# A two-layer hybrid decoder step on one core: the scale before the shift, the first tiles from x without the shift

## The chip, the cores and the metric

The kernel runs on one core of one Trainium2 chip. The time is device microseconds of one execution. The kernel before took 1080.2 us (median of three runs, 1079.94 to 1081.06).

## The reference, cut to what matters

The step takes 512 prompt rows and 8 sample rows through two layers. The change touches the beginning of the first layer and, through the order of its weights, the modulation of both. In float32:

```python
def rmsnorm(x, g):
    y = xf * rsqrt(mean(xf * xf, axis=-1) + EPS)
    return y * g

def adaln(c, w, b):                       # shift, scale, gate: 1024 columns each
    mod = (silu(c) @ w + b)[:, None, :]
    return split(mod, 3, axis=-1)

def even_layer(x, c, g, aw, ab, w_in, ...):
    shift, scale, gate = adaln(c, aw, ab)
    h = rmsnorm(x, g) * (1 + scale) + shift
    z = h @ w_in                          # 8 x 1024 columns
    bg, cg, xv, ga, q, k, v, gb = split_cols(z, ...)
    ...                                   # short convolution; dilated attention of 16 heads
    out = concatenate([y_a, y_b]) @ w_out
    return x + gate * out
```

The prompt has one vector c, the eight samples have one each, so shift and scale are nine rows. The prompt's row multiplies all 512 positions.

## The kernel before

**Layout.** Everything is kept by feature: a tile has 128 features on the partitions and 520 positions (512 prompt, 8 sample) beside each other. x is eight such tiles, xT[0..7]. A product tile of z is 128 columns of w_in times the eight tiles of h. It is made in full float32 precision by three passes: weights and input are each split into a high half (rounded by ACT, `whi` and the first of each pair in `h0`) and a low half (the difference, made by DVE). For each k in 0..7, `mm3` issues six matrix instructions (three passes, positions 0 to 255 and 256 to 519 apart), so a tile has 48. Product tiles lie in PSUM in a pool of two buffers (`mm`); everything else on PSUM shares four (`aux`). ACT evicts the prompt's part of a tile, DVE the samples' (`sample_z`).

**Modulation.** `ada_load` fetches a 1 MB block of the modulation weights into one of three `big` buffers. Before, a block "ss" holds the shift and the scale of one k. `ada_mm` multiplies it with silu(c) (`scT`, eight products, 16 instructions), ACT copies the rows out (`md`), `ada_fin` transposes them on PE, and DVE reduces them (`m9`) to the columns `mS` (shift) and `mA` ((1 + scale) times the norm's weight).

**The head.** SP issues all loads in the order of the program: c, the eight x tiles, two small tables, then modulation blocks and weight tiles. ACT squares the x tiles, DVE adds the squares, PE multiplies them with a 128 x 128 matrix of 1/1024 (lines 407 to 409), so that every partition has the mean; ACT takes the root, DVE the reciprocal (r0), and POOL multiplies the eight x tiles by it (line 416). The loop over j (lines 422 to 448) then does for each k: the modulation block, `h_hi` and `h_lo` (scale and shift x, split it), and the products of the first two tiles (v and k of head pair 0) with h of k = j - 2.

**The pairs.** `head_pair(p)` makes four tiles for two heads: v, k, gate, q. The weights come in the order `seq`. The attention of pair p is put into the products of pair p + 1 by ticks: a tick is the end of one k of a tile (six instructions), so a tile has eight and a pair 32. `at(n, f)` runs f n ticks later; `put` queues work for PE that runs at one piece a tick from its due tick on. For a pair they are the scores (`score`, four blocks of queries), biased by DVE, made exponentials and normalised by ACT and DVE; the transposes of the weights (`turn`, six groups; ACT copies a high half, DVE makes the low half a tick later); and the products with v (`weigh`, eight). The first scores are due five ticks (`Q0`) after the pair's four tiles, the first transposes 16 ticks after them.

Each engine takes its instructions in the order of the program; what stands behind a waiting one waits too.

## Time and profile before

| | |
|---|---|
| median of three runs | 1080.2 us |
| the profiled execution | 1080.08 us, its span 1078.3 |
| PE busy | 1042.2 us of the span (97%), 8656 instructions |
| DVE, ACT, POOL busy | 638.1, 492.3, 27.4 us |
| moved from and to HBM | 149.40 MB read, 18.65 MB written |
| first two product tiles end | 51.41 us into the span |
| pairs 2 to 6, each | 33.4 us |

A window row shows where an engine is short of work, and the granted clock in it. A row of the chain of waits gives a piece that nothing else could overlap. A group row gives the mean duration of a kind of instruction. A duration counts from an instruction's start to its end; of two behind each other on ACT the second may start about 0.1 us before the first ends.

### The profile page before, as it was taken

What the parts mean: (1) busy time and instruction counts of PE and PEld (TensorE: products, weight loads), DVE (VectorE), ACT (ScalarE), POOL (GpSimd) and SP (SyncE); (2) the same over time, 40 slices, a digit from 0 to 9 for tenths busy, and PEclk for the clock granted to TensorE, in tenths of its full rate; (3) what the DMA queues carried; (4) which work ended last, traced back from release to release, by engine and by line L of the source; (5) the groups of instructions that cost most, each with busy time, mean ns of one, the idle gap of its engine ahead of it and who ended that gap; (6) DMA issues with size and microseconds to landing.
All of it is one profiled execution on the core that took longest, in us unless ns stands there. A gap on an engine that the chain in (4) does not pass through costs nothing.

```text
span 1078.3 us, 21052 instructions
## 1 busy us (share of the span) xinstructions
PE 1042.2 (97%) x8656; PEld 989.0 (92%) x8656; DVE 638.1 (59%) x1468; ACT 492.3 (46%) x890; POOL 27.4 (3%) x45
## 2 busy tenths in 40 slices
PE   3999999999999999999999989999999999999996
PEld 1699999999989999999999989999999999999996
DVE  6556777667786444446344586565647666674443
ACT  4575667656663222223333465435454444333333
POOL 3000000000000000000000040000000000000000
PEclk9999999999999999999999999999999999999999
DMA  9486545665436355352744335272635423225212
GB/s 356 159 271 189 166 143 161 209 185 181 141 129 195 119 198 159 117 170 91 248 160 150 105 118 195 91 253 98 235 123 178 171 96 109 83 81 181 99 70 80
DMA packets 82177, 168.96 MB, mean 157 GB/s; under 512 B 7209, under 2 KB 47241, under 8 KB 79001
## 3 DMA queue, kind: packets, MB, share of 16 engines
q1 hardware_dynamic: 82080, 167.61, 46.6%
q8 instruction: 68, 1.11, 0.4%
q14 instruction: 29, 0.23, 0.1%
HBM read 149.40 MB, written 18.65 MB: 156 GB/s over the span
## 4 chain that ended last, share of the span: by engine, by line
PE 92%; DVE 4%; ACT 2%; DMA 1%; issue 1%; SPq 0%; DVEq 0%; ACTq 0%
PE mm L160 75%; PE aux L160 13%; PE aux L543 2%; DVE t L146 1%; ACT t L140 1%; DVE wlo L146 1%; DMA v<-vdr 1%; PE aux L348 0%; PE aux L1239 0%; DVE t L149 0%; DMA t<-in_x_t 0%; PE aux L463 0%; DVE t L202 0%; PE aux L918 0%; ACT whi L140 0%
## 5 line engine op out<-in xcount | busy, mean ns | idle before, releaser
L160 PE MATMUL mm<-t,whi 128*128 128x256 f32 (+1 forms) x4608 | 764.5, 287 | 7.1 <-ACT t L140 4.9
L160 PEld LDWEIGHTS mm<-t,whi 128*128 128x128 f32 x4608 | 637.3, 189 | 36.2 <-issue 21.9
L160 PE MATMUL mm<-t,wlo 128*128 128x256 f32 (+2 forms) x2304 | 465.7, 282 | 0.0
L160 PEld LDWEIGHTS mm<-t,wlo 128*128 128x128 f32 x2304 | 358.8, 189 | 0.0
L146 DVE TENSOR_TENSOR wlo<-wraw,whi 128x512 fp32r<-128x512 f32 x288 | 192.6, 699 | 52.0 <-ACT whi L140 51.7
L140 ACT ACTIVATE whi<-wraw 128x1024 fp32r<-128x1024 f32 x144 | 151.6, 1053 | 98.1 <-PE mm L160 62.9
L146 DVE TENSOR_TENSOR t<-t,t 128x520 fp32r<-128x520 f32 (+6 forms) x164 | 107.0, 652 | 96.3 <-ACT t L140 94.6
L140 ACT ACTIVATE t<-t 128x520 fp32r<-128x520 f32 (+3 forms) x116 | 70.9, 616 | 166.0 <-DVE t L149 97.8
L140 ACT ACTIVATE t<-aux 128x128 f32<-128x128 f32 (+7 forms) x148 | 67.9, 469 | 115.9 <-PE aux L160 64.8
L140 ACT ACTIVATE t<-mm 128x512 f32<-128x512 f32 (+2 forms) x116 | 56.4, 507 | 114.0 <-PE mm L160 112.5
L146 DVE TENSOR_TENSOR t<-aux,t 128x512 fp32r<-128x512 f32 (+6 forms) x120 | 60.8, 512 | 37.1 <-ACT t L140 32.0
L160 PE MATMUL aux<-t,t 64*128 64x256 f32 (+6 forms) x384 | 56.2, 329 | 0.0
L160 PE MATMUL aux<-t,v 128*128 128x512 f32 (+2 forms) x224 | 49.1, 324 | 0.6 <-DVE t L146 0.6
L521 DVE CUSTOM_DVE_ANT_0 t<-aux,t 128x128 f32<-128x128 f32 (+3 forms) x64 | 28.9, 489 | 31.9 <-PE aux L160 31.4
L160 PEld LDWEIGHTS aux<-t,t 64*128 64x128 f32 (+1 forms) x384 | 41.5, 186 | 5.4
L140 ACT ACT_TABLE_LOAD x32 | 41.1, 1283 | 1.3 <-PEq L1353 0.7
L140 ACT ACTIVATE t<-t,mn 128x128 f32<-128x128 f32 (+3 forms) x64 | 35.4, 554 | 13.3 <-DVE mn L521 13.1
L160 PEld LDWEIGHTS aux<-t,v 128*128 128x128 f32 x224 | 34.4, 188 | 1.9 <-DVE t L146 0.8
L149 DVE SCALAR_TENSOR_TENSOR big<-v,ksc,big 128x256 f32<-128x256 f32 x64 | 27.7, 480 | 10.3 <-ACT big L140 9.9
L350 DVE TENSOR_REDUCE m<-aux 128x18 f32<-128x72 f32 x24 | 5.5, 231 | 45.8 <-PE aux L348 45.8
L143 DVE COPY zs<-mm 128x8 f32<-128x8 f32 x76 | 12.1, 159 | 34.6 <-ACT t L140 33.7
L146 DVE TENSOR_TENSOR t<-mm,t 128x512 f32<-128x512 f32 (+1 forms) x24 | 16.5, 689 | 26.6 <-PE mm L160 17.4
(145 smaller groups left out, 603.2 us busy)
## 6 DMA issues: line engine op xcount, KB each, us to landing
wraw<-in_w_in_e SPq DMA_DIRECT2D x64, 512.0 KB, 6.4
wraw<-in_w_in_o SPq DMA_DIRECT2D x48, 512.0 KB, 3.2
big<-in_ada_e SPq DMA_DIRECT2D x12, 1024.0 KB, 8.3
big<-in_ada_o SPq DMA_DIRECT2D x12, 1024.0 KB, 8.5
wraw<-in_w_out_e SPq DMA_DIRECT2D x16, 512.0 KB, 3.5
big<-in_state_ret SPq DMA_DIRECT2D x16, 512.0 KB, 7.5
out_new_ret_sample<-big SPq DMA_DIRECT2D x16, 512.0 KB, 3.7
wraw<-in_w_out_o SPq DMA_DIRECT2D x16, 512.0 KB, 3.2
```

What stands on the lines that cost most here:

```text
L140: return nc.scalar.activation(out=out, in_=in_, func=func, scale=scale, **kw)
L143: return nc.vector.tensor_copy(out, in_)
L146: return nc.vector.tensor_tensor(out=out, in0=in0, in1=in1, op=op)
L149: return nc.vector.scalar_tensor_tensor(out=out, in0=in0, scalar=scalar, in1=in1, op0=op0, op1=op1)
L160: nc.tensor.matmul(out, lhsT=lhsT, rhs=rhs, start=start, stop=stop)
L350: nc.vector.tensor_reduce(out=m, in_=pt.rearrange("p s (g r) -> p s r g", g=4)[:, :, 0:9, :], op=ALU.add, axis=AX.X)
L521: nc.vector.tensor_tensor_reduce(out=sb, in0=s[:, 0:n], in1=bt[e][:, S - n:S], scale=1.0, scalar=3e38, op0=ALU.add, op1=ALU.min, accum_out=mn,
L543: nc.tensor.transpose(ep[:, c * P:(c + 1) * P], src, ident)
```

## The change

The modulation weights are stored in three parts now, scale, shift and gate, in blocks of two k each. So four blocks give the scale of all eight k, four more the shift.

x is loaded ahead of the rest and squared; the mean is now taken by five products with one column, the root and its reciprocal on 5 columns, and turned back into rows by products of the broadcast column with the identity (`rms_rows`). DVE multiplies each x tile by r0 (`x_normed`). `x_scaled` scales x by `mA` and splits it, without the shift; the first four tiles (pair 0) are made of that (`xa`). The shift blocks are multiplied among the products of the third and fourth tile (`steps`). In pair 1 the raw weights of the first four tiles (kept in `t4` buffers, `raw_of`) are multiplied with the shift (`shift_rows`, `z_shift`), and the result is added to the kept tiles. The four tiles of pair 1 are made of the x without shift too, with ten more columns that hold the shift (`z_second`, 530 instead of 520 columns). During pair 1, `h_x` adds the shift to x in place, and `h_split` splits it anew into the same `xa` buffers, at ticks 8 to 22 and 25 to 32. From pair 2 on everything is as before. The work of pair 0's attention is moved by D0 = 8 ticks.

```diff
-            r = mk(wp, [P, KT, P], F32, "wraw", 4)
+            r = t4().rearrange("p (k c) -> p k c", k=KT) if i < 4 else mk(wp, [P, KT, P], F32, "wraw", 4)
+            raw_of.append(r)
...
+    def rms_sums(sq, n=T):
+        blocks = [c * P for c in range(n // P)] + ([n - P] if n % P else [])
+        pc = aux([P, len(blocks)])
+        for i, c in enumerate(blocks):
+            mm(pc[:, i:i + 1], sq[:, c:c + P], on_d[:, 0:1], True, True)
+        return pc
+    def rms_roots(pc, scale=1.0):
+        rc = mk(cp, [P, 5], F32, "rc", 2)[:, 0:pc.shape[1]]
+        act(rc, pc, ACTF.Sqrt, bias=eps[:, 0:1], scale=scale)
+        nc.vector.reciprocal(rc, rc)
+        return rc
+    def rms_rows(rc, r):
+        pr, n = aux([P, S]), r.shape[1]
+        for i in range(4):
+            mm(pr[:, i * P:(i + 1) * P], rc[:, i:i + 1].to_broadcast([P, P]), ident, True, True)
+        act(r[:, 0:S], pr)
+        if n > S:
+            pr = aux([P, n - S])
+            mm(pr, rc[:, 4:5].to_broadcast([P, P]), ident[:, P - n + S:P], True, True)
+            vcopy(r[:, S:n], pr)
...
+    load(csm[:, 0:P], a["c_small"][:, 0:P])
     xT = [tt() for _ in range(KT)]
     for j in range(KT):
         load(xT[j], a["x_t"][:, j, :])
-    load(csm[:, 0:P], a["c_small"][:, 0:P])
-    load(pv, a["small_t"])
-    raw0 = [ada_load(0, "ss", 0)]
-    w_raw()
-    raw0.append(ada_load(0, "ss", 1))
-    w_raw()
-    raw0.append(ada_load(0, "ss", 2))
+        if j == 1:
+            load(pv, a["small_t"])
...
+    rawA = []
+    for i in range(3):
+        rawA.append(ada_load(0, "scale", i))
+        if i < 2:
+            w_raw()
...
-    for x in xT:
-        nc.gpsimd.tensor_tensor(out=x, in0=x, in1=r0, op=ALU.mult)
...
+    rms_rows(rms_roots(rms_sums(sqa)), r0)
+    def x_normed(j):
+        vtt(xT[j], xT[j], r0, ALU.mult)
+    def x_scaled(j):
+        x, g = xT[j], mA[0][:, j, 8:9]
+        hi, lo = tr(T + 10), tr(T + 10)
+        vtt(xhs[:, j, :], x[:, S:T], mA[0][:, j, 0:NB], ALU.mult)
+        act(hi[:, 0:S], x[:, 0:S], ACTF.Copy, scale=g)
+        act(hi[:, S:T], xhs[:, j, :])
+        stt(lo[:, 0:S], x[:, 0:S], g, f(hi[:, 0:S]), ALU.mult, ALU.subtract)
+        lo_of(lo[:, S:T], xhs[:, j, :], hi[:, S:T])
+        xa.append((hi, lo))
...
+    md = ada_mm(rawA[0])
+    x_normed(0)
+    x_normed(1)
+    ada_fin(0, "scale", 0, md)
+    for i in range(4):
+        for j in (2 * i, 2 * i + 1):
+            x_scaled(j)
+        for _ in range((2, 0, 1, 0)[i]):
             w_hi()
             w_lo()
+        if i == 0:
+            rawA.append(ada_load(0, "scale", 3))
+        else:
+            rawS.append(ada_load(0, "shift", i - 1))
+            w_raw()
+        if i < 3:
+            x_normed(2 * i + 2)
+            x_normed(2 * i + 3)
+            if i:
+                first_two(2 * i)
+            md = ada_mm(rawA[i + 1])
+            first_two(2 * i + 1 if i else 0)
+            ada_fin(0, "scale", i + 1, md)
+            if i == 0:
+                first_two(1)
+        else:
+            first_two(6)
+            first_two(7)
+    for (_, _, m), ps in zip(seq, ps01):
+        z_keep(m, ps)
...
+    def shift_fin(i):
+        ada_fin(0, "shift", i, mdS.pop(i))
+        for j in (2 * i, 2 * i + 1):
+            act(xa[j][0][:, T:T + 10], mS[0][:, j, :])
+            lo_of(xa[j][1][:, T:T + 10], mS[0][:, j, :], xa[j][0][:, T:T + 10])
+        if i < 1:
+            rawS.append(ada_load(0, "shift", 3))
+            w_raw()
+    mdS = {}
+    steps = {
+        (2, 0): [w_hi], (2, 1): [w_lo, lambda: shift_mm(0)], (2, 3): [lambda: shift_fin(0)],
+        (2, 4): [lambda: shift_mm(1)], (2, 6): [lambda: shift_fin(1), w_raw],
+        (2, 7): [lambda: shift_mm(2)], (3, 1): [lambda: shift_fin(2)],
+        (3, 2): [w_hi], (3, 3): [w_lo, lambda: shift_mm(3)], (3, 5): [lambda: shift_fin(3), w_raw],
+        (3, 6): [w_hi], (3, 7): [w_lo],
+    }
+    for t in (2, 3):
+        ps, w = mm2(), take_w(seq[t])
+        for k in range(KT):
+            mm3(ps, w, k, xa[k][0], xa[k][1], k == 0, k == KT - 1)
+            for fn in steps.get((t, k), ()):
+                fn()
+        z_keep(seq[t][2], ps)
...
+    def shift_rows(n):
+        at(1, z_shift, n, rows_mm(scS, raw_of[n].unsqueeze(2)))
+    def z_shift(n, md):
+        m, x = zf[n]
+        ws = rows_turn(md)
+        act(x, x, ACTF.Silu if n == 2 else ACTF.Identity, bias=ws[:, 0, 8:9])
+        vtt(zs[0][:, m, :], zs[0][:, m, :], ws[:, 0, 0:NB], ALU.add)
+    for n in range(4):
+        at(1 + 2 * n, shift_rows, n)
+    h0 = xa
+    def h_x(j):
+        x = xT[j]
+        vtt(x[:, S:T], xhs[:, j, :], mS[0][:, j, 0:NB], ALU.add)
+        act(x[:, 0:S], x[:, 0:S], ACTF.Identity, scale=mA[0][:, j, 8:9], bias=mS[0][:, j, 8:9])
+    def h_split(j):
+        hi, lo = xa[j]
+        act(hi[:, 0:T], xT[j])
+        lo_of(lo[:, 0:T], xT[j], hi[:, 0:T])
+    for j in range(KT):
+        at(8 + 2 * j, h_x, j)
+        at(25 + j, h_split, j)
+    def z_second(m, func=ACTF.Identity):
+        ps = z_tile(0, m, xa, T + 10)
+        x, ws = tt(S), mk(cp, [P, 9], F32, "ws", 2)
+        vcopy(ws, ps[:, 1, T - H0:T - H0 + 9])
+        act(p2(x), ps[:, :, 0:H0], func, bias=ws[:, 8:9])
+        vtt(zs[0][:, m, :], ps[:, 1, H0:H0 + NB], ws[:, 0:NB], ALU.add)
+        return x
...
+        if p == 0:
+            D0 = 8
+            put_fill(v_out, zf[0][1], after=4)
+            at(6, k_made, zf[1][1])
+            st["sg"] = zf[2][1]
+            at(9, lambda: q_made(p2(zf[3][1])))
+            at(7, bias_load)
+            at(11, window_load)
+        elif p == 1:
+            D0 = 0
+            put_fill(v_out, z_second(48 + p), after=2)
+            at(1, k_made, z_second(40 + p))
+            st["sg"] = z_second(56 + p, ACTF.Silu)
+            bias_load()
+            at(5, window_load)
+            q_made(p2(z_second(32 + p)))
...
+            put(score, qb, after=D0 + Q0 + n)
```

The engines' instructions stand in another order at three places. First PE at the start of the program. Before, the four products with the matrix `on_d` come first, then three modulation blocks (`aux<-big`) with their transposes (`aux<-csm,md`), and then the first products with `whi`:

```order
L160 MATMUL aux_159<-t_137,on_d 128x256
L160 MATMUL aux_160<-t_137,on_d 128x264
L160 MATMUL aux_159<-t_157,on_d 128x256
L160 MATMUL aux_160<-t_157,on_d 128x264
L160 MATMUL aux_182<-big_125,scT 32x256 x8
L348 MATMUL aux_195<-csm,md_191 128x128 x2
L160 MATMUL aux_207<-big_129,scT 32x256 x8
L348 MATMUL aux_226<-csm,md_216 128x128 x2
L160 MATMUL aux_240<-big_133,scT 32x256 x8
L160 MATMUL mm_180<-t_222,whi_193 128x256
```

After, on PE at the same place:

```order
L160 MATMUL aux_165<-on_d,t_140 128x1 x5
L160 MATMUL aux_174<-csm,rc_171 128x128 x4
L160 MATMUL aux_180<-csm,rc_171 128x8
L160 MATMUL aux_185<-big_126,scT 32x256 x8
L354 MATMUL aux_198<-csm,md_194 128x128 x2
L160 MATMUL aux_233<-big_130,scT 32x256 x8
L160 MATMUL mm_183<-t_205,whi_219 128x256
```

The first products now follow the second block, and the broadcast of r0 stands ahead of the first.

Second, ACT in pair 1, from the last exponentials of pair 0 up to the eviction of the first transposes. Before (`t_827` and `t_829` are the fourth block's weights of the two heads, `t_898<-aux` is the eviction, `v_850` is the split of v):

```order
L140 ACTIVATE whi_813<-wraw_661 128x1024
L140 ACTIVATE t_763<-t_763,ls_732 128x256
L140 ACTIVATE t_765<-t_765,ls_736 128x256
L140 ACTIVATE t_827,ls_732<-t_827,mn_731 128x512
L140 ACTIVATE t_829,ls_736<-t_829,mn_735 128x512
L140 ACTIVATE t_848<-aux_843 128x512
L140 ACTIVATE v_850<-t_848 128x8x64
L140 ACTIVATE t_827<-t_827,ls_732 128x512
L140 ACTIVATE t_829<-t_829,ls_736 128x512
L140 ACTIVATE t_898<-aux_893 128x512
```

After (`t_1006` and `t_1008` are those weights, `t_114` to `t_116` are x tiles of `h_x`, `t_1020` is the key's split of pair 1):

```order
L140 ACTIVATE whi_990<-wraw_771 128x1024
L140 ACTIVATE t_114<-t_114,mS_88,mA_86 128x512
L140 ACTIVATE t_934<-t_934,ls_891 128x256
L140 ACTIVATE t_936<-t_936,ls_895 128x256
L140 ACTIVATE t_1020<-t_969 128x512
L140 ACTIVATE t_1006,ls_891<-t_1006,mn_890 128x512
L140 ACTIVATE t_1008,ls_895<-t_1008,mn_894 128x512
L140 ACTIVATE t_115<-t_115,mS_88,mA_86 128x512
L140 ACTIVATE t_1006<-t_1006,ls_891 128x512
L140 ACTIVATE t_1008<-t_1008,ls_895 128x512
L140 ACTIVATE t_116<-t_116,mS_88,mA_86 128x512
L140 ACTIVATE t_1074<-aux_1069 128x512
```

Three x tiles and a key split stand among them now; one more x tile (`t_113`) stands between the first exponentials and these rows.

Third, DVE in the same pair, among the low halves of the transposed weights (`t<-aux,t`) and the window scores (`big`). Before, from the first low half to the fifth (`t_973`):

```order
L146 TENSOR_TENSOR t_899<-aux_893,t_898 128x512
L573 TENSOR_REDUCE t_518<-big_649 128x8x2
L146 TENSOR_TENSOR t_921<-aux_915,t_920 128x512
L146 TENSOR_TENSOR big_649<-big_649,v_775 128x1024
L146 TENSOR_TENSOR t_937<-aux_932,t_936 128x384
L573 TENSOR_REDUCE t_518<-big_649 128x8x2
L146 TENSOR_TENSOR wlo_964<-wraw_675,whi_929 128x512
L146 TENSOR_TENSOR t_956<-aux_951,t_955 128x384
L146 TENSOR_TENSOR wlo_964<-wraw_675,whi_929 128x512
L146 TENSOR_TENSOR t_947<-t_902,t_946 128x512
L146 TENSOR_TENSOR t_973<-aux_967,t_972 128x512
```

After, from the second low half of x (`t_213`) to the fifth of the weights (`t_1159`); ahead of these rows stand the first low half of x (`t_206`), the first of the weights and a window sum:

```order
L146 TENSOR_TENSOR t_213<-t_110,t_212 128x520
L146 TENSOR_TENSOR t_1104<-aux_1098,t_1103 128x512
L146 TENSOR_TENSOR big_854<-big_854,v_948 128x1024
L146 TENSOR_TENSOR t_276<-t_111,t_275 128x520
L146 TENSOR_TENSOR t_1122<-aux_1117,t_1121 128x384
L698 TENSOR_REDUCE t_671<-big_854 128x8x2
L146 TENSOR_TENSOR wlo_1148<-wraw_808,whi_1112 128x512
L146 TENSOR_TENSOR t_283<-t_112,t_282 128x520
L146 TENSOR_TENSOR t_1140<-aux_1135,t_1139 128x384
L146 TENSOR_TENSOR wlo_1148<-wraw_808,whi_1112 128x512
L146 TENSOR_TENSOR t_338<-t_113,t_337 128x520
L146 TENSOR_TENSOR t_1159<-aux_1153,t_1158 128x512
```

Low halves of x stand between those of the weights, five ahead of the fifth.

More of the change, by code (lines that the diff above doesn't have):

```diff
@@ L231, in hybrid_kernel @@
     nc.gpsimd.memset(zer, 0.0)
-    nc.gpsimd.memset(mS[1], 0.0)
+    for t in mS:
+        nc.gpsimd.memset(t, 0.0)
     nc.gpsimd.memset(eps, EPS)
@@ L352, in ada_fin, with ada_mm @@
         )
-        if kind == "ss":
-            vts(mS[layer][:, j, 0:9], m[:, 0, :], pvc(f"ada{layer}", j), None, ALU.add)
-            vts(mA[layer][:, j, :], m[:, 1, :], bsc[layer][:, j:j + 1], pvc(f"norm{layer}", j), ALU.add, ALU.mult)
-        else:
-            for s in range(2):
-                vts(mG[layer][:, 2 * j + s, :], m[:, s, :], pvc(f"ada{layer}", 16 + 2 * j + s), None, ALU.add)
+        return m
+    def ada_mm(raw):
+        return rows_mm(scT, raw)
+    def ada_fin(layer, kind, i, md):
+        m = rows_turn(md)
+        for s in range(2):
+            j = 2 * i + s
+            if kind == "scale":
+                vts(mA[layer][:, j, :], m[:, s, :], bsc[layer][:, j:j + 1], pvc(f"norm{layer}", j), ALU.add, ALU.mult)
+            elif kind == "shift":
+                vts(mS[layer][:, j, 0:9], m[:, s, :], pvc(f"ada{layer}", j), None, ALU.add)
+            else:
+                vts(mG[layer][:, j, :], m[:, s, :], pvc(f"ada{layer}", 16 + j), None, ALU.add)
     def ada(layer, kind, j, raw=None):
@@ L404, in hybrid_kernel @@
         act(sq, xT[j], ACTF.Square)
-        if 0 < j < KT - 1:
+        if j > 0:
             vtt(sqa, sqa, sq, ALU.add)
-    ssq, r0 = [aux([P, 512]) for _ in range(2)], tt()
-    for x, first in ((sqa, True), (sq, False)):
-        mm(ssq[0][:, 0:H0], on_d, x[:, 0:H0], first, not first)
-        mm(ssq[1][:, 0:T - H0], on_d, x[:, H0:T], first, not first)
-    act(r0[:, 0:H0], ssq[0][:, 0:H0], ACTF.Sqrt, bias=eps[:, 0:1])
-    act(r0[:, H0:T], ssq[1][:, 0:T - H0], ACTF.Sqrt, bias=eps[:, 0:1])
@@ new lines, in first_two, with z_keep @@
+    def first_two(k):
+        if not w01:
+            w01.extend((take_w(seq[0]), take_w(seq[1])))
+        for w, ps in zip(w01, ps01):
+            mm3(ps, w, k, xa[k][0], xa[k][1], k == 0, k == KT - 1)
+    rawS, zf = [], []
+    def z_keep(m, ps):
+        x = tt(S)
+        act(p2(x), ps[:, :, 0:H0])
+        sample_z(0, m, ps)
+        zf.append((m, x))
+    md = ada_mm(rawA[0])
[6 more added lines that the diff above has]
+        for _ in range((2, 0, 1, 0)[i]):
@@ L493, in window_load @@
             st["kw"] = kw
-            raw = ada_load(1, "ss", p)
-            at(20, ada, 1, "ss", p, raw)
+            kind = ("scale", "shift")[p // 4]
+            raw = ada_load(1, kind, p % 4)
+            at(20, ada, 1, kind, p % 4, raw)
         def q_load():
@@ L608, in head_pair, with k_made, gate_made, q_made @@
-        at(1, q_lo)
+        def k_made(kf):
+            load(o["k_t"][p], kf)
+            at(2, k_split, kf)
+        def gate_made(src):
+            st["sg"] = sg = tt(S)
+            act(p2(sg), src, ACTF.Silu)
+        def q_made(src, after=None):
+            qh, ql = tr(S), tr(S)
+            st["q"] = (qh, ql)
+            act(p2(qh), src, ACTF.Copy, scale=-0.125)
+            def q_lo():
+                stt(p2(ql), src, -0.125, p2(f(qh)), ALU.mult, ALU.subtract)
+                if after:
+                    after()
+            at(1, q_lo)
@@ L837, in hybrid_kernel @@
         if m < 4:
-            at(14, ada, 1, "g", m, ada_load(1, "g", m))
+            at(14, ada, 1, "gate", m, ada_load(1, "gate", m))
         if m == KT - 1:
```

145 lines of the change are left out of this document (56 added, 89 removed).

## The prediction, made before the run

> **What bounds the kernel now.** I read the page first, then a table of windows cut at the places where the work changes, then the chain that ended last.
>
> ```profile
> span 1078.3 us, 21052 instructions
> ...
> PE 92%; DVE 4%; ACT 2%; DMA 1%; issue 1%; SPq 0%; DVEq 0%; ACTq 0%
> ```
> ```profile
> 0.00:10.72 10.72, 0.00 (x0) 0.03 (x1) 4.20 (x6) 8.11 (x13) 0.94 (x9) 1.00 0.81 280
> 10.72:25.70 14.98, 8.12 (x61) 4.34 (x61) 11.41 (x13) 4.17 (x8) 8.02 (x6) 0.88 1.01 413
> 25.70:32.50 6.80, 5.24 (x30) 3.65 (x30) 6.23 (x13) 2.61 (x4) 3.75 (x4) 0.51 0.17 67
> 32.50:51.41 18.91, 17.97 (x162) 13.37 (x158) 9.61 (x35) 11.62 (x19) 0.00 (x0) 1.00 0.53 211
> 51.58:63.63 12.05, 12.05 (x101) 12.05 (x102) 5.42 (x10) 7.06 (x9) 0.00 (x0) 1.00 0.72 225
> 63.63:97.05 33.42, 33.42 (x280) 31.05 (x279) 22.17 (x57) 21.93 (x43) 0.00 (x0) 1.00 0.67 220
> ```
>
> The columns are the window and its length, the busy time of PE, PE's weight loads, DVE, ACT and POOL, the granted clock, and the DMA. The chain is PE for 92%. PE idles or runs at half clock (0.51) only in the first rows; from 51.58 it is busy without a gap, through the two last tiles of pair 0 (to 63.63) and through pair 1 (33.42 us). So time can be won only ahead of 51.41, where the first two tiles end. Behind it, every microsecond that PE gets more of, or waits, is added to the end.
>
> **The head before.** The next lines are pieces of the chain (start, length, what) and then rows of the timeline and of the groups.
>
> ```profile
> 9.87 0.71 DVE t L146
> 15.94 1.66 DVE t L414
> 38.61 1.85 PE mm L160 x12
> 40.46 0.22 PE aux L348 x2
> 40.68 1.00 PE aux L160 x16
> 53.71 12.91 PE mm L160 x108
> ```
> ```profile
> 7.54 2.67 ACT L140 ACTIVATE t<-t 128x520 f32<-128x520 f32 x4 [0.23 <-DMA t<-in_x_t]
> 10.72 3.81 PE L160 MATMUL aux<-t,on_d 128*128 128x256 f32 x8 [10.72 <-DVE t L146]
> 20.22 1.07 PE L160 MATMUL aux<-big,scT 128*32 128x256 f32 x16 [1.44 <-DMA big<-in_ada_e]
> ```
> ```profile
> L416 POOL TENSOR_TENSOR t<-t,t 128x520 f32<-128x520 f32 x8 | 11.5, 1473 | 16.2 <-DVE t L414 16.2
> L160 PE MATMUL aux<-on_d,t 128*128 128x1 f32 x2 | 0.4, 246 | 0.5 <-DVE t L146 0.5
> L350 DVE TENSOR_REDUCE m<-aux 128x18 f32<-128x72 f32 x6 | 1.4, 233 | 7.2 <-PE aux L348 7.2
> L154 DVE TENSOR_SCALAR mA<-m,bsc,pv 128x9 f32<-128x9 f32 x6 | 1.7, 285 | 0.0
> L140 ACT ACTIVATE t<-t,ls 128x512 f32<-128x512 f32 x2 | 1.3, 718 | 0.0
> L149 DVE SCALAR_TENSOR_TENSOR t<-mm,t 128x512 fp32r<-128x512 f32 x1 | 0.7, 690 | 2.8 <-ACT t L140 2.8
> L140 ACT ACTIVATE whi<-wraw 128x1024 fp32r<-128x1024 f32 x4 | 4.2, 1050 | 0.0
> L146 DVE TENSOR_TENSOR wlo<-wraw,whi 128x512 fp32r<-128x512 f32 x8 | 5.2, 683 | 0.2 <-ACT whi L140 0.2
> ```
>
> The last row of the chain gives the unit: 108 products in 12.91 us, 0.12 us each, so a tile of 48 takes 5.74. A modulation block takes 1.00 for its products and 0.31 up to the end of its transposes (40.46 to 40.68, and the wait ahead): 1.31. Before, all eight blocks stand ahead of 51.41; after, four do.
>
> **The head after (my walk).** The last square ends at 10.21 (7.54 + 2.67). Two small loads now stand among the x loads; at the 280 to 413 GB/s of the windows their 116 KB take 0.4. The last addition (0.71) then ends at 11.4 instead of 10.59. Root and rows: five one-column products (pairs of 0.35, some 1.5 together), root and reciprocal 0.5, four 128-column products, each half of the 256-column one (3.81 / 8 = 0.48, so 0.24, two instructions each: 1.9), eviction 0.6: r0 stands at 16.1; before at 17.6. Two x tiles by DVE (0.7 each) end at 17.5; POOL's 1.47 each is gone. The first scale block is behind the rows on PE; its reduce and mA (0.23, 0.29) end at 18.6. ACT then has two scaled copies (0.72) with small ones, and two whi (1.05): 21.6 for the first. DVE's four wlo halves end at 24.2, two more x tiles at 25.6.
>
> From here a cycle per pair of k: reduce and mA 0.6, scaled copy 0.72, its difference 0.69, ten products 1.2, a scale block 1.0, twelve products 1.45, transposes 0.3: 6.1. Two cycles, 0.2 more for the third weight tile on DVE, bring the last transposes to 38.0; then 0.6 + 0.72 + 0.69 + 22 products and small waits end the two tiles at 42.8. That is at full clock. At half clock for the first 4 us it is 44.1. I take **43.5: −7.9**. Bounds: −11 (the start 2 us earlier, nothing late) and −5.5 (r0 and the weights later by 2).
>
> The row 25.70:32.50 shows the clock at 0.51 though PE had worked until 21.3 (20.22 + 1.07). The Trainium skill ("TensorE: Matmul & The Clock Gate", Part 1) says that PE falls to half rate after an idle window of about 3.4 us. By that rule PE's pause in my walk, some 2 us ahead of 21.6, would leave the clock full and the sum would be 0.7 lower.
>
> **What moves behind the head.** Four shift blocks between the products of the third and fourth tile: 4 × 1.31 = **+5.2**. PE has no gap there now, so nothing hides them. The shift's own products with the four raw weight tiles, 16 instructions of 128 columns each, four times:
>
> ```profile
> L160 PE MATMUL aux<-big,scT 128*32 128x256 f32 x384 | 26.7, 397 | 2.3 <-DMA big<-in_ada_e 1.4 <-DVE t L146 0.9
> L160 PE MATMUL aux<-big,pT 128*32 128x512 f32 x64 | 7.7, 598 | 0.0
> ```
>
> Per instruction that is 0.070 at 256 columns and 0.12 at 512; half of 0.07 at 128 is the lower bound, 0.07 the upper. With a transpose (0.15): 0.7 to 1.25 each; I take 0.95, **+3.8** (2.8 to 5). [...] Ten more columns for the 96 products of the second pair: +0.4. So PE alone: −7.9 + 5.2 + 3.8 + 0.4 = +1.5. The loads hide: four shift loads and weights follow the scale loads while the DMA share is 0.53 or less, and each has at least one 6 us cycle.
>
> **What DVE and ACT get in pair 1.** This is the term that decides. In pair 1 the eight x tiles are shifted in place on ACT (h_x) and split anew on ACT and DVE (h_split), beside the attention of pair 0.
>
> ```profile
> L140 ACT ACTIVATE t<-t,mS,mA 128x512 f32<-128x512 f32 x8 | 6.5, 808 | 3.0 <-DVE mA L154 3.0
> L140 ACT ACTIVATE t<-t 128x520 fp32r<-128x520 f32 x8 | 5.1, 638 | 7.2 <-DVE t L146 7.0
> L146 DVE TENSOR_TENSOR t<-t,t 128x520 fp32r<-128x520 f32 x7 | 4.9, 694 | 0.8 <-ACT t L140 0.8
> ```
> ```profile
> 67.37 0.62 PE L160 MATMUL aux<-t,t 64*128 64x256 f32 x6
> 68.36 0.40 ACT L140 ACTIVATE t<-t,mn 128x128 f32<-128x128 f32 x1
> 78.03 1.34 ACT L140 ACTIVATE t<-t,ls 128x512 f32<-128x512 f32 x2
> 79.09 0.60 PE L543 MATMUL aux<-csm,t 128*128 128x128 f32 x4
> 87.84 1.28 ACT L140 ACT_TABLE_LOAD   x1
> 88.24 1.28 DVE L146 TENSOR_TENSOR t<-aux,t 128x512 fp32r<-128x512 f32 x2
> 90.01 0.40 PE L160 MATMUL aux<-t,v 128*128 128x256 f32 x2
> ```
> ```profile
> ACT t L140 <- DVE mn L521: 1.6, 2, 1.4
> ```
>
> Read them as one race. After the first scores (67.37, ended 67.99) ACT makes the exponentials and norms. The first of the last two norms, which the first transposition needs, ends near 78.75; PE issues it at 79.09, 11.1 after the scores. ACT has only 1.6 + 0.3 us to spare. After, between the same two points stand the ops for k 4 to 6 of h_x and a key split: 3 × 0.71 + 0.53 (about 0.1 less than the listed 0.81 and 0.63 back to back, as 1.34 for two of 0.72 shows). Moreover ACT comes late to the first exponential. From tick 8 of the pair (0.4 ahead of it) it has four h_x, the key split, the last shift of pair 0, an eviction, the query, a whi and the table load, 7.5 in all, while the first scores and DVE's work on them are through 5.0 after that tick (five ticks of 0.72, the scores 0.62, the bias on DVE). So it starts 2.1 late. Late 2.1 + added 2.7 − spare 1.9 = **2.8 us of waiting for PE** at the first transposition. PE queues everything in order behind it: pair 1's last tile first.
>
> Second race: the low halves of the transposed weights. Before, the fifth ends near 88.9 (two in 88.24 + 1.28), 9.8 after 79.09, and the product that needs it starts at 90.01, 1.1 later; PE fills that stretch with a modulation block (1.31) that falls behind it after the change. So DVE has no room. After, five low halves of x (0.6 each back to back, 3.0) are queued ahead of the fifth. The first of them waits for its high half on ACT, and that stands behind the table load (1.28), an eviction, the gate's silu and the last h_x, some 3.2 in which DVE has nothing to do. The key's low half (0.6) and 1.1 of window work lie in front now. 9.8 + 3.0 + 3.2 − 0.6 − 1.1 = 14.3 from the first transposition to the fifth low half; PE could come there in 9.7. **4.6 us more.** The transposes in between also wait for their aux buffers, inside the same 4.6. Pile-up: **+7.4**. It is bounded below by 4.0 (the five low halves and 1 of the first race) and above by 9.5 (both, and the weight split behind them late by 2).
>
> Later pairs are as before, and PE has no gap there to take the loss back.
>
> **Sum.** The profiled execution took 1080.08, with 1078.3 of span; the median of the runs is 1080.2, so it stands for them. 1080.1 + 1.5 + 7.4 = **1089.0**. With all lower bounds −11 + 5.2 + 2.8 + 0.4 + 4.0 = +1.4, 1081.5; with all upper ones −5.5 + 5.2 + 5 + 0.4 + 9.5 = +14.6, 1094.7.
>
> **Rivals.**
> - *The pile-up is hidden.* If ACT is through with the fourth norm when PE is at the transposition, the h_x ops fell into real gaps. For it: ACT's busy time in pair 1 is 21.93 of 33.42, and 14 more would still fit the sum. Against it: the two races above, in which the room counts and not the share. Price −7.4, so 1081.6 with the head at 43.5. **It is faster than before when the first two tiles also end before 41.5**: −9.9 in the head gives 1079.6, with the shift's products at their lower bound 1078.6, and at the head's lower bound 1077.5. The point that decides is PE's wait ahead of the first transposition of pair 0: under 0.5 us or not.
> - *Half of it.* ACT is on time, but DVE's queue still delays the fifth low half by 3, with the head at −9.9: 1082.6. With the shift's products at the lower bound, 1081.6, within 0.2%.
> - *The head isn't shorter.* x and its root come first, but the scale blocks still go one by one through reduce, scaled copy, difference and product. If r0 or the weight splits come 4 us later than in my walk, the two tiles end at 47.5, and the sum is 1093.
>
> **How the numbers follow.** A measurement of this kernel tells some 0.2% (2.2 us) from no change. Forecast (pile-up of 4 to 9.5): 0.66. Hidden pile-up: 0.16, two thirds of it faster. Half: 0.10, mostly within. Head not shorter: 0.08. Of the forecast's own chance 0.06 goes to its lower end, within 0.2%, and 0.02 to faster. Faster 0.13, same 0.17, slower 0.70. The range runs from 1080 to 1094.
>
> **What would show it.** First two tiles ending near 43.5 with a clock of 0.5 or 1.0 at the first products; third and fourth tile with four blocks among them in 16.8 instead of 12.05; pair 1 some 6 us longer than 33.42 and pair 2 some 5, with PE idle ahead of the first group of L668 transposes (released by ACT) and ahead of the third product of the weighing (released by DVE). Were PE busy without a gap in that pair, the 7.4 would be wrong; were the first two tiles to end at 40 or at 47, the walk through the head would be.

## The result, and the profile after

| | before | after |
|---|---|---|
| median of four runs | 1080.18 us | 1097.12 us (1096.90 to 1097.34) |
| ratio, 95% interval | | 1.0154 (1.0141 to 1.0167) |
| span of the profiled execution | 1078.3 | 1095.6 |
| third tile starts | 51.58 | 47.73 |
| pair 1 starts | 63.63 | 65.18 |
| pair 3's part of `out_k_t` is stored | 147.67 | 163.57 |

The change makes the kernel 16.9 us slower. The direction was as forecast; the size was not, 1097.1 instead of 1089.0, and above the range.

The page's span and the shares of its chain:

```profile
span 1095.6 us, 21274 instructions
...
PE 89%; DVE 5%; ACT 4%; issue 1%; DMA 0%; SPq 0%; DVEq 0%; ACTq 0%
```

PE has 3% less of the chain than before (89 instead of 92), DVE and ACT together have 3% more: what grew isn't only work on PE, but waiting. Where, the windows show, cut at the places at which the work changes (columns as in the prediction):

```profile
12.65:24.00 11.35, 7.87 (x54) 5.60 (x54) 4.11 (x13) 3.75 (x9) 0.00 (x0) 0.96 0.90 358
24.00:28.00 4.00, 3.85 (x18) 3.86 (x19) 3.86 (x7) 1.31 (x3) 0.00 (x0) 0.50 0.90 357
28.00:32.00 4.00, 4.00 (x34) 3.69 (x37) 3.42 (x10) 1.65 (x4) 0.00 (x0) 0.75 0.04 15
32.00:36.00 4.00, 2.59 (x27) 1.94 (x20) 0.97 (x5) 1.33 (x4) 0.00 (x0) 1.00 0.57 207
36.00:40.00 4.00, 3.72 (x24) 2.81 (x28) 3.52 (x9) 1.65 (x3) 0.00 (x0) 0.60 0.46 188
...
47.73:65.18 17.45, 17.45 (x170) 14.55 (x171) 6.53 (x26) 6.28 (x17) 0.00 (x0) 1.00 0.46 169
65.18:106.70 41.52, 36.89 (x319) 33.26 (x319) 25.68 (x77) 36.75 (x70) 0.00 (x0) 0.96 0.67 203
106.70:146.40 39.70, 37.48 (x310) 33.81 (x310) 30.23 (x74) 24.69 (x48) 0.00 (x0) 1.00 0.54 160
146.40:179.80 33.40, 33.40 (x278) 30.99 (x277) 23.48 (x59) 21.92 (x43) 0.00 (x0) 1.00 0.48 157
```

Read from below: pair 3 takes 33.40, as before. Pair 1 is 8.1 longer than its 33.42 and pair 2 6.3 longer, and PE is not busy for 4.63 and 2.22 of that. Tiles 3 and 4 take 17.45 instead of 12.05, without a gap. In the head the granted clock is at half in two stretches, from 24 to about 30 and for most of the row from 36.

The chain through the head (start, length, what):

```profile
12.65 2.28 PE aux L160 x10
...
15.50 4.21 PE aux L160 x26
...
23.15 0.96 ACT whi L140
24.14 2.97 PE mm L160 x12
...
36.62 2.39 PE mm L160 x10
39.01 1.61 PE aux L160 x16
...
44.67 2.19 PE mm L160 x16
```

The one-column sums are PE's first work and take 2.28; the ten products of k = 4 and the last block behind them take 4.0, nearly all of it at half clock, from 36.62 to 40.62. Rows of PE's timeline ahead of k = 4 and of k = 6, and at the start of the third tile (a bracket gives the idle time ahead and what ended it):

```profile
35.83 0.51 PE L160 MATMUL mm<-t,whi 128*128 128x256 f32 x2 [1.41 <-ACT t L140]
36.62 0.66 PE L160 MATMUL mm<-t,whi 128*128 128x256 f32 x2 [0.28 <-DVE t L149]
...
43.88 0.50 PE L160 MATMUL mm<-t,whi 128*128 128x256 f32 x2 [1.41 <-ACT t L140]
44.67 0.51 PE L160 MATMUL mm<-t,whi 128*128 128x256 f32 x2 [0.28 <-DVE t L149]
...
47.73 0.74 PE L160 MATMUL mm<-t,whi 128*128 128x256 f32 x4 [0.18 <-DVE zs L143]
```

The waits of PE between 60 and 180:

```profile
PE aux L160 <- DVE t L146: 3.1, 3, 1.9
PE aux L668 <- ACT t L140: 2.2, 1, 2.2
PE aux L160 <- issue: 1.3, 1, 1.3
PE aux L668 <- DVE t L146: 0.2, 1, 0.2
```

Rows of PE's timeline for them:

```profile
67.22 0.65 PE L160 MATMUL aux<-v,t 128*32 128x128 f32 x16 [1.32 <-issue]
...
94.78 0.46 PE L668 MATMUL aux<-csm,t 128*128 128x128 f32 x1 [2.22 <-ACT t L140]
94.89 1.23 PE L160 MATMUL mm<-t,whi 128*128 128x256 f32 x4
...
97.07 1.23 PE L160 MATMUL mm<-t,whi 128*128 128x256 f32 x4
...
98.67 0.73 PE L160 MATMUL mm<-t,whi 128*128 128x256 f32 x4
...
105.08 0.70 PE L160 MATMUL aux<-t,v 128*128 128x512 f32 x2 [0.85 <-DVE t L146]
...
109.60 0.38 PE L160 MATMUL aux<-t,v 128*128 128x256 f32 x1 [1.90 <-DVE t L146]
109.82 0.65 PE L160 MATMUL mm<-t,whi 128*128 128x256 f32 x4
```

The 2.22 at the first transposes and the 1.90 at the weighing are the two waits that the prediction named, with the engines that it named. Two things in these rows it did not name: the 1.32 ahead of the first products with the shift, and four products in 1.23 instead of some 0.7, for 3.8 us from 94.89. For the first, DVE's timeline:

```profile
65.64 1.29 DVE L146 TENSOR_TENSOR wlo<-wraw,whi 128x512 fp32r<-128x512 f32 x2 [0.78 <-ACT whi L140]
...
66.93 0.19 DVE L143 COPY t<-mS 128x72 f32<-128x72 f32 x1
```

The copy of the shift into its padded operand (`scS`) stands behind two low halves of a weight tile, and PE starts 0.1 after its end: "issue" in the row of waits is this.

### The profile page after: what moved, and what is told of

Its sections match the earlier page's. It is cut to its first block, busy times and chain, and to the rows that moved or that the text cites. A ratio compares the mean times of both kernels' runs of the same rounds, so it can differ in the third digit from the quotient of the medians.

```text
span 1095.6 us, 21274 instructions
## 1 busy us (share of the span) xinstructions
PE 1053.7 (96%) x8736; PEld 999.9 (91%) x8736; DVE 642.4 (59%) x1514; ACT 503.8 (46%) x924; POOL 16.3 (1%) x39
## 4 chain that ended last, share of the span: by engine, by line
PE 89%; DVE 5%; ACT 4%; issue 1%; DMA 0%; SPq 0%; DVEq 0%; ACTq 0%
PE mm L160 72%; PE aux L160 13%; ACT t L140 3%; DVE t L146 1%; PE aux L668 1%; DVE wlo L146 1%; ACT whi L140 1%; DVE t L149 1%; PE aux L354 1%; DMA t<-in_x_t 0%; PE aux L1395 0%; ACT L140 0%; SPq L157 0%; PE aux L1067 0%; PE aux L1074 0%
## 5 line engine op out<-in xcount | busy, mean ns | idle before, releaser
L160 PE MATMUL mm<-t,whi 128*128 128x256 f32 (+2 forms) x4608 | 768.4, 289 | 6.1 <-ACT t L140 2.8
L146 DVE TENSOR_TENSOR wlo<-wraw,whi 128x512 fp32r<-128x512 f32 x280 | 185.8, 693 | 51.0 <-ACT whi L140 50.2
L140 ACT ACTIVATE whi<-wraw 128x1024 fp32r<-128x1024 f32 x140 | 147.6, 1054 | 97.9 <-PE mm L160 63.5
L146 DVE TENSOR_TENSOR t<-t,t 128x520 fp32r<-128x520 f32 (+7 forms) x181 | 114.1, 634 | 92.5 <-ACT t L140 90.7
L140 ACT ACTIVATE t<-t 128x520 fp32r<-128x520 f32 (+4 forms) x126 | 73.9, 592 | 161.7 <-DVE t L149 98.0
L140 ACT ACTIVATE t<-aux 128x512 f32<-128x512 f32 (+7 forms) x149 | 68.6, 470 | 105.9 <-PE aux L160 60.3
L356 DVE TENSOR_REDUCE m<-aux 128x18 f32<-128x72 f32 (+1 forms) x28 | 6.4, 228 | 47.9 <-PE aux L354 47.9
L140 ACT ACTIVATE md<-aux 128x256 f32<-128x256 f32 (+1 forms) x28 | 10.3, 367 | 46.6 <-PE aux L160 46.6
```

The source lines that it names most:

```text
L140: return nc.scalar.activation(out=out, in_=in_, func=func, scale=scale, **kw)
L146: return nc.vector.tensor_tensor(out=out, in0=in0, in1=in1, op=op)
L160: nc.tensor.matmul(out, lhsT=lhsT, rhs=rhs, start=start, stop=stop)
L356: nc.vector.tensor_reduce(out=m, in_=pt.rearrange("p s (g r) -> p s r g", g=4)[:, :, 0:9, :], op=ALU.add, axis=AX.X)
```

## The experiments

Each was run beside the kernel before on the same chip (medians of it: 1080.4 to 1080.9). The profiled execution is one of the timed ones and can lie a microsecond or two from the median; times below are medians.

**1. Without the replacement of x.** The pairs from the third on are then made of x without the shift.

```diff
-    for j in range(KT):
-        at(8 + 2 * j, h_x, j)
-        at(25 + j, h_split, j)
```

> The changed kernel without h_x and h_split: x is neither shifted in place nor split anew in pair 1, so pairs 2 to 7 and the tiles behind them are made of x without the shift. Theory (the pile-up on ACT and DVE makes PE wait 5.2 us at the transposes and the weighing of pair 0, and about 1.5 us more go to the halved clock behind the first of these waits): 1097.1 falls to about 1090.4, and PE waits at neither place. Rival (the time lies in what PE itself has more to do): less than 2 us won, above 1095.

1091.69 us (1090.66 to 1092.68), ratio 1.0102 (1.0087 to 1.0117). So the pile-up costs 5.4 us: the theory holds against its rival, with 1.3 less than it said. PE's waits between 60 and 180 in this run:

```profile
PE aux L160 <- issue: 1.3, 1, 1.3
PE aux L160 <- DVE t L146: 0.7, 1, 0.7
PE aux L665 <- DVE t L146: 0.7, 1, 0.7
PE aux L665 <- ACT t L140: 0.4, 1, 0.4
```

Of the 6.8 of waiting 3.7 are gone, and with them the half clock behind the transposes (the granted clock is 1.00 from 92 to 110). 3.1 are left that stand there without the replacement too: 1.3 for the copy of the shift and, other than the theory said, 1.8 at the transposes and the weighing. The kernel is still 11 us slower than before: the larger part of the loss isn't the pile-up.

**2. Without the scale and shift of x in place, with the new split.**

```diff
-        at(8 + 2 * j, h_x, j)
         at(25 + j, h_split, j)
```

> The changed kernel without h_x alone (the eight ops on ACT that add the shift to x in place, and their eight small ones on DVE); x is still split anew, so pairs 2 to 7 get x without scale and shift. Theory (two races one behind the other): the wait ahead of the first transposes, 2.2 us, and the halved clock behind it go, the second race on DVE stays: 1093 to 1094. Rival (one race, DVE's): the wait moves to the weighing and the time stays within 1 us of 1097.

1097.66 (1096.62 to 1098.09), ratio 1.0156: nothing is gained, and the theory of two races that add up falls. The waits show why:

```profile
PE aux L160 <- DVE t L146: 3.1, 3, 1.9
PE aux L667 <- DVE t L146: 2.4, 2, 2.2
...
PE aux L667 <- ACT t L140: 0.4, 1, 0.4
```

ACT comes in time at the first transposes (0.4 instead of 2.2), and now DVE is late by 2.2 at a later group of them (99.91), ahead of which PE had no wait before; its waits for DVE at the weighing and behind it are the same 3.1. What PE wins at the first race it loses at DVE's queue 6.5 us later. The granted clock stays full behind the first transposes here, and the time doesn't gain by that either.

**3. Full clock in the head of the changed kernel.** Dummy products (of a constant with itself, read by nobody) in PE's idle times: 42 ahead of the sums, 9 behind the second block, 5 to 7 ahead of k = 2, 4 and 6.

```diff
+    def busy(n):
+        ps = aux([P, P])
+        for _ in range(n):
+            mm(ps, on_d, on_d, True, True)
...
+    busy(42)
     rms_rows(rms_roots(rms_sums(sqa)), r0)
...
```

> The changed kernel with products of a constant with itself, read by nobody, put into PE's waits in the head: 42 ahead of the means, 9 ahead of the first tile products, 5, 7 and 7 ahead of k = 2, 4 and 6. Theory (the halved clock makes the head 4 us longer than my walk: 1.2 in the root and rows, 0.9 in the first scale block, 1.5 and 1.0 in the first products, 1.7 in the cycle of k = 4 and 5): the granted clock stays at 1.00 and the first two tiles end near 43 instead of 47.5; the kernel takes 1092 to 1093. Rival (the pauses come from the chain through ACT and DVE and not from the clock): no gain, 1097, or some more for the added products.

1094.55 (1093.05 to 1095.25), ratio 1.0127 (1.0111 to 1.0142). The theory holds against its rival, but it gains less than it said (1092 to 1093, third tile near 43):

```profile
44.90 0.75 PE L160 MATMUL mm<-t,whi 128*128 128x256 f32 x4 [0.18 <-DVE zs L143]
```

The third tile starts at 44.90 instead of 47.73, and the time follows by 2.6. The clock wasn't full throughout: it was at half from 15.0 to 18.4. The profiled runs that leave the head as it is (the changed kernel, and experiments 1, 2, 6 and 7) start the third tile between 46.31 and 49.54, so this start lies outside their spread. From k = 4's first scaled copy to k = 6's it takes 6.52 (33.74 to 40.26 in the chain), instead of 8.05 (35.06 to 43.11) after.

**4. The same in the kernel before** (36 ahead of the mean, 5 ahead of the third block, 16 ahead of the first products).

> The kernel before with such products in its own waits: 36 ahead of the means, 5 ahead of the third block, 16 ahead of the first tile products. Theory (its head ran at half clock from 22 to 32): the products and blocks of that stretch take 2 to 3 us less and the means 1.5 less: 1076 to 1078. Rival (that stretch is set by DVE, which POOL slows): within 1 us of 1080.2.

1079.87 (1079.14 to 1081.08), ratio 0.9993 (0.9983 to 1.0003). The third tile starts 1.2 earlier (50.39), the time doesn't change beyond its uncertainty. The clock is full there (1.00 from 6 to 50), and still PE's products wait, 2.3 for DVE between 10 and 51: its rows are slow in the kernel before, as experiment 9 shows.

**5. Small loads behind x, and the two additions that need them behind the mean.**

```diff
-    load(csm[:, 0:P], a["c_small"][:, 0:P])
     xT = [tt() for _ in range(KT)]
     for j in range(KT):
         load(xT[j], a["x_t"][:, j, :])
-        if j == 1:
-            load(pv, a["small_t"])
+    load(csm[:, 0:P], a["c_small"][:, 0:P])
+    load(pv, a["small_t"])
...
```

> The changed kernel with its two small loads (identity, small tables) behind all x tiles, and the two small additions that need the table behind the mean instead of ahead of it. In the trace after, x's last square ended 0.8 us and the sum of squares 1.2 us later than in the walk of the prediction, and the two loads stand between the x tiles. Theory: the chain from x to the first tiles' products starts 1.0 us earlier and carries it through: third tile at 46.7 instead of 47.7, time about 1096.1. Rival: the first scale block, the weight tiles or the half clock set the start, so that an earlier sum only lengthens a wait: third tile within 0.3 of 47.7, time within 0.4 of 1097.1.

1095.56 (1094.87 to 1096.95), ratio 1.0137. By the time alone the theory holds; by the trace the sum of squares is ready only 0.5 earlier (12.05 instead of 12.51) and the third tile starts at 47.33. So the loads account for 0.5 of the 1.1 by which the sum came later than in the walk; where the rest comes from was not taken apart. This run settles little: executions of it spread over 2 us.

**6. The shift copied early**, in pieces, as soon as each pair of k is made.

```diff
         ada_fin(0, "shift", i, mdS.pop(i))
+        vcopy(scS[:, 2 * i:2 * i + 2, 0:9], mS[0][:, 2 * i:2 * i + 2, 0:9])
...
-    vcopy(scS[:, :, 0:9], mS[0][:, :, 0:9])
```

> The changed kernel, but each pair of k of the shift is copied into the padded operand of the shift's products as soon as it is made, among the products of the third and fourth tile, instead of all at once behind them. Theory: PE's wait of 1.32 us at the start of pair 1 came from that one copy queued on DVE behind the low halves of a weight tile; it goes, and all that follows in pair 1 moves with it: time about 1096.0, the later waits (2.2 at the transposes, 1.9 at the weighing) unchanged to 0.3. Rival: as with the run that left the shift of x out, the time comes back as a longer wait for DVE at the weighing, and the time stays within 0.4 of 1097.1.

1095.08 (1094.37 to 1095.55), ratio 1.0134. The wait of 1.32 is gone, the later ones are the same (2.2 and 3.1 in the waits), and PE keeps the lead: from the start of the third tile to pair 3's store it takes 1.4 less than after (46.31 to 160.72 against 47.73 to 163.57). The theory holds. The medians differ by 2.0; the 0.6 that is left isn't explained by the edit: the head, which it doesn't touch, was 1.4 shorter in this execution.

**7. The replacement spread over pairs 1 and 2.**

```diff
-        elif p == 1:
+        elif p in (1, 2):
...
-        at(8 + 2 * j, h_x, j)
-        at(25 + j, h_split, j)
+        at(8 + 6 * j, h_x, j)
+        at(57 + j, h_split, j)
```

> The changed kernel, with pair 2 made of the unshifted x too (530 columns and the shift's columns added at eviction), so that the shift of x in place is spread over six ticks each in pairs 1 and 2, and the new split follows the last tile of pair 2. The amount of work on ACT and DVE is the same, PE has 0.4 us more (ten more columns for another 192 products) and all outputs are the same. Theory: the 6.7 us of pile-up are a matter of where the replacement stands, not of how much work it is; about 5 to 6 us go, time 1091 to 1092, as with the replacement left out (1091.7). Rival: ACT and DVE lack the room anywhere in these pairs: the waits reappear in pair 2 at the transposes and the weighing there, and the time is 1095 or more.

1096.80 (1095.92 to 1100.03), ratio 1.0156: nothing is gained, against the theory. (The profiled execution is the slowest of the four, its third tile starts at 49.54; from there to the end it takes 0.9 more than the changed kernel.) In pair 1 the waits sink to 1.8 at the transposes (1.1 for ACT, 0.7 for DVE) and 0.7 at the weighing; but PE waits 3.5 us at the end of pair 2 for DVE, which reaches the samples' sum (`zs`) only behind eight low halves of x.

**8. All repairs together** (5, 6, 7 and the dummy products of 3), then once more with that transposition of pair 2's samples six ticks later.

```diff
-        put_fill(q_rows, after=D0 + 4)
+        put_fill(q_rows, after=D0 + (10 if p == 2 else 4))
```

> The changed kernel with all four repairs at once: small loads behind x, shift copied early, replacement spread over pairs 1 and 2, and dummy products that keep the clock full through the head. Theory: the terms are mostly separate: 1097.1 - 1.0 - 1.2 - 5.5 - 2.6 = about 1087, still slower than the kernel before, since the four shift blocks (5.2) and the shift's products (3.8) on PE outweigh a head that is shortened by some 8. Rival: the terms are coupled (a lead that PE wins early is lost again at the next wait for DVE), so that the sum is 1090 or more. If it were under 1082, the price of the shift's products would be overstated.

> The run with all four repairs, with one thing more: the transposition of pair 2's sample queries is put six ticks later, since the spread replacement itself made PE wait 3.5 us there (DVE reached the samples' sum of pair 2 only behind eight low halves of x). Theory: that wait and the slow products behind it go, and what is left follows from the terms: third tile 7.4 earlier than before, tiles 3 and 4 5.4 longer, shift's products 3.8, columns 0.8, waits left some 2.6, 1 of later drift: about 6 above the kernel before, 1086 to 1088.5. Rival: the replacement costs DVE and ACT time that has no place in either pair, and the wait comes up again at the next product that needs DVE: 1091 or more.

1093.69 (1092.57 to 1094.76), ratio 1.0122, and 1091.20 (1090.44 to 1094.81), ratio 1.0101 (1.0087 to 1.0116). Both times the rival holds. In the last run the third tile starts at 42.73, 8.9 earlier than before, and the lead is used up and more: the wait has come up again at the next place that needs DVE. PE's, ACT's and DVE's rows there:

```profile
142.26 1.32 PE L160 MATMUL aux<-t,t 64*128 64x256 f32 x6 [3.28 <-ACT t L140]
```
```profile
140.86 0.69 ACT L140 ACTIVATE t<-mm,ws 128x512 f32<-128x512 f32 x1 [4.49 <-DVE ws L143]
```
```profile
138.61 1.30 DVE L146 TENSOR_TENSOR t<-t,t 128x520 fp32r<-128x520 f32 x2
139.93 0.69 DVE L146 TENSOR_TENSOR t<-aux,t 64x512 f32<-64x512 f32 x1
140.65 0.17 DVE L143 COPY ws<-mm 128x9 f32<-128x9 f32 x1
```

Read backwards: PE's scores wait for ACT, which evicts the query tile only when DVE has copied its shift's columns (`ws`), a copy of 0.17 that stands behind the last low halves of x. ACT idles 4.49 for it. DVE is in order, and at each of the places that were tried in these pairs the low halves of x stood ahead of something that PE needs.

**9. The kernel before with the start of the change alone**: the mean by one-column products (`rms_sums`, `rms_roots`, `rms_rows`), and x multiplied by DVE, two tiles ahead, instead of POOL. All eight modulation blocks, with the shift, stay in the head.

```diff
...
-    for x in xT:
-        nc.gpsimd.tensor_tensor(out=x, in0=x, in1=r0, op=ALU.mult)
+    rms_rows(rms_roots(rms_sums(sqa)), r0)
+    def x_normed(j):
+        vtt(xT[j], xT[j], r0, ALU.mult)
+    x_normed(0)
+    x_normed(1)
...
+        if j + 2 < KT:
+            x_normed(j + 2)
```

> The kernel before with the head's mean and normalisation alone taken from the change: one-column sums, five roots and reciprocals, rows by the identity, and DVE instead of POOL multiplying x by r0, two tiles ahead; the modulation blocks, the shift and all tiles stay as before. Theory: with POOL's multiplications gone DVE's small instructions and weight halves take 0.28 and 0.6 us again instead of about 1.3, so the chain to the first products is some 2 us shorter (third tile near 49.5 instead of 51.6): 1077 to 1079. Rival: the first products wait for the weights and the clock and not for DVE, and DVE's own 0.65 per tile eats the gain: within 1 us of the kernel before.

**1075.56** (1074.85 to 1076.72), ratio 0.9948 (0.9935 to 0.9962): faster than both kernels, and by more than expected. The third tile starts at 48.00. The changed kernel, which puts only half of the modulation ahead of it, starts it at 47.73. DVE's rows, of the kernel before:

```profile
18.91 1.32 DVE L154 TENSOR_SCALAR mA<-m,bsc,pv 128x9 f32<-128x9 f32 x1
20.14 2.37 DVE L146 TENSOR_TENSOR wlo<-wraw,whi 128x512 fp32r<-128x512 f32 x2
22.44 1.24 DVE L146 TENSOR_TENSOR t<-t,mA 128x8 f32<-128x8 f32 x1
```

and of this run:

```profile
20.85 0.28 DVE L154 TENSOR_SCALAR mA<-m,bsc,pv 128x9 f32<-128x9 f32 x1
21.04 1.28 DVE L146 TENSOR_TENSOR wlo<-wraw,whi 128x512 fp32r<-128x512 f32 x2
...
22.86 0.16 DVE L146 TENSOR_TENSOR t<-t,mA 128x8 f32<-128x8 f32 x1
```

The same instructions on the same shapes take 0.28 instead of 1.32, 1.28 instead of 2.37 (for two), 0.16 instead of 1.24 when POOL isn't multiplying beside them. The kernel before shows the same by itself: POOL multiplies from 17.68 to 29.17, and from 30 on these forms take 0.28 and 0.16 there too. The edit replaces the mean as well, and the two were not tried apart; but r0 is complete at 17.60 in the kernel before and not earlier here (17.75), so that up to there the new mean won nothing.

**10. The same with dummy products**, first at all three places (42 ahead of the sums, 9 behind each of the first two blocks, 16 ahead of the first products), then 36 ahead of the sums alone.

> The same kernel with dummy products in PE's idle times of the head (42 ahead of the sums, 9 behind each of the first two modulation blocks, 16 ahead of the first products) that keep the granted clock at 1. Theory: in the kernel before the dummy products alone gave 1.2 us in the third tile's start, since DVE set the stretch; with DVE free of POOL they add to it: third tile near 47.5 to 48.5, 1075.5 to 1077.5. Rival: no more than the run without them: then the clock's half rate overlaps a wait that is there anyway.

> The kernel with the head's mean and normalisation alone (the one that took 1075.6), and dummy products at one place only: 36 of them ahead of the sums, in time in which PE has nothing to do; those between the modulation blocks and ahead of the first products, which PE had to finish before its next work (2.17, 2.17 and 3.84 us), are left out. Theory: the clock is full at the sums, so that sums, rows and the first two blocks take half as long as cold (2.27, 2.30, 1.94 and 1.94 become 1.2, 1.3, 1.07 and 1.07) and the chain starts some 2 us earlier; PE's pauses behind are below 1 us and keep the clock: third tile near 46.3 instead of 48.0, 1073 to 1074.5. Rival: the first products then wait for the weights' halves on DVE and ACT instead, and the time is 1075 or more.

1079.19 (1078.02 to 1080.07), ratio 0.9984 (0.9975 to 0.9993), which is slower than without them and misses both theories: the products stand in front of PE's next work and have to end first (the 16 took 3.84, the 9 took 2.17 each; the third tile starts at 50.10). Which of the places cost how much was not tried apart. With those ahead of the sums alone **1074.11** (1073.19 to 1075.70), ratio 0.9946 (0.9932 to 0.9959). PE's rows of that run:

```profile
11.59 1.28 PE L160 MATMUL aux<-on_d,t 128*128 128x1 f32 x10 [0.37 <-DVE t L146]
13.44 1.28 PE L160 MATMUL aux<-csm,rc 128*128 128x128 f32 x10 [0.58 <-DVE rc L394]
```
```profile
44.51 0.74 PE L160 MATMUL mm<-t,whi 128*128 128x256 f32 x4 [0.17 <-DVE zs L143]
```

The sums take 1.28 instead of 2.27, the rows 1.28 instead of 2.30, and in the profiled execution the third tile starts at 44.51, 7.1 earlier than before. The time is where the theory had it, with the third tile 1.8 earlier than it said. Against the run without dummy products the medians differ by 1.5 and the ratios' intervals overlap, so that the two are not told apart for certain; both beat the kernel before.

## Why the prediction was right in sign and wrong in size

All in the profiled executions, span against span: 17.3 measured, 8.9 predicted.

| step | predicted | measured |
|---|---|---|
| first two tiles end earlier | −7.9 | −3.85 |
| shift blocks in tiles 3 and 4 | +5.2 | +5.4 |
| pairs 1 and 2: shift's products and columns | +4.2 | |
| pairs 1 and 2: pile-up | +7.4 | |
| pairs 1 and 2 together | +11.6 | +14.35 |
| from pair 3 to the end | 0 | +1.4 |

- **The head: the term that was mis-sized.** The walk took "−7.9" and allowed half clock "for the first 4 us" only. Measured −3.85, outside its bound of −5.5. Two steps failed. The start: the sum of squares stood at 12.5 instead of 11.4, and sums and rows, PE's first work, took 2.27 and 2.30 instead of 1.5 and 1.9; so the first high half of the weights ended at 24.1 instead of 21.6. And the cycle: the walk's 6.1 (its terms add up to 5.96) was 8.05 for k = 4, since PE waited 1.41 for ACT and 0.28 for DVE, with two products between, and then ran at half clock. Experiment 3 shows the second and part of the first directly: with dummy products the third tile starts at 44.90, 6.7 earlier than before and inside the walk's bounds, and that cycle takes 6.52. The late sum of squares stays (12.74 there). The rival "the head isn't shorter" named this outcome, 47.5 and 1093, and of the cause only the late weights (2.5 us, not 4); the half clock in the cycle it did not name.
- **Four shift blocks in tiles 3 and 4: right in kind, dearer than said.** The two tiles took 5.4 more for the predicted 5.2, and nothing hid the blocks. But the four transposes of pair 0's v (0.60 in the rows, at 53.11 before) moved out of this stretch into pair 1 (71.09 after), so that the blocks themselves cost some 6.0. That the forecast comes so near is partly luck.
- **The shift's products: right.** 16 instructions take 0.65 in the row at 67.22, and the next product starts 0.58 after the first of them, 0.036 for each; from one group of 16 to the next it is 2.35 (67.22 to 69.57) with twelve ordinary products of 0.12 in it, so a group with its transpose costs some 0.9. The term was 0.95.
- **The pile-up: places and engines right, its make-up wrong.** Taking the replacement away gave 5.4, for 7.4 predicted and bounds of 4.0 and 9.5. PE waited for ACT ahead of the first transposes (2.22 for 2.8) and for DVE at the weighing (0.85 and 1.90 for 4.6). But the prediction added the two, "2.8 + 4.6" (the first is 2.9 by its own terms), and experiment 2 shows that they do not add: without the first PE meets DVE's queue earlier and waits there. The waits that went with the replacement are only 3.7, under the lower bound; some 1.5 of the 5.4 is half clock, which the sum did not have. That 5.4 lies inside the bounds is partly luck.
- **What was left out.** PE's wait of 1.32 for the copy of the shift (experiment 6: its removal is kept); half clock behind the 2.22 pause, some 1.5 by the rows from 94.89 to 98.67 against the same rows at full clock; the 0.6 of the moved transposes; and 1.8 of waits at transposes and weighing that stay when the replacement is gone (experiment 1), which were not taken apart.
- **Open.** In pairs 1 and 2 some 1.3 us of PE's time have no row of their own: 14.35, less 4.2 of products (the predicted 3.8 + 0.4, of which the rows bear out the first), 6.8 of waits, 1.5 of half clock and 0.6 of transposes. And 1.4 us accrue slowly behind pair 3, most of it up to 600 us, in stretches where the program is the same; experiment 1's run shows 1.1 of it, experiment 10's last run nothing. Experiment 4's run, the same program as before behind the head, loses 0.5 in the same way between 350 and 540. It was not explained.

The sign, too, is explained differently than by the pile-up alone. With all repairs the changed kernel needs 1091.2; with only the start of the change the kernel before needs 1075.6. Ahead of the third tile PE, DVE and ACT take turns, and the four shift blocks fitted into PE's gaps there: the third tile starts at 48.00 with them and 47.73 without, and with dummy products ahead at 44.51 with them (experiment 10) and 44.90 without (experiment 3). Behind the third tile the kernel of experiment 9 takes as long as the kernel before (1026.9 and 1026.7 in the profiled spans). Moved there, the blocks and the products that make up for the missing shift cost their full price, 5.4 more in tiles 3 and 4 and some 4.2 in the pairs.

## What to carry to other kernels

Work that is moved out of a latency-bound start is free there only if it was what the start waited for; look for the engine that ends the waits (here DVE, slowed by POOL, and a PE at half clock) before deferring another one's work. A later stage in which one engine is busy without a gap pays the full price for what is moved into it, and in-order neighbours with spare time by their busy share can have none at the place where it counts. A repair that only moves such work along the queue, or takes away the first of several waits, should be expected to meet the next dependent instruction: experiments 2, 7 and 8 did here.
